# Modulation rows of a hybrid diffusion block: the four products of a weight tile in one burst

## The chip, the core and the metric

The kernel runs on one core of one Trainium2 chip. The metric is the device time of one launch, in microseconds (us). Profiles are one execution each, taken by the hardware profiler.

## What is computed

One layer of a hybrid step over 384 tokens (128 context, 256 latent) of width 2048, all in fp32. Cut to what matters here:

```python
mod_ctx = silu(c_ctx) @ ada_w + ada_b          # ada_w: 2048 x 6144
mod_lat = silu(c)     @ ada_w + ada_b
shift, scale, gate = split(mod, 3)             # 2048 columns each
h   = rmsnorm(x, norm_g) * (1 + scale) + shift
z   = h @ w_in                                 # the big projection, 2048 x 20864
...                                            # two-way scans (branch A), short convolution (branch B)
out = (sigmoid(m_a) * (y_a @ w_out_a) + sigmoid(m_b) * (y_b @ w_out_b)) @ w_o
x   = x + gate * out                           # then a last norm
```

The change touches only the first two lines, the products of the two conditioning rows with `ada_w`: the shift and scale columns in the prologue, the gate columns near the end.

## The kernel before

**Two rows against a wide matrix.** The two conditioning rows, as columns, are the stationary operand: `cw[:, k, :]` is 128 x 32, of which two columns are used. The moving operand is a loaded tile `raw` of `ada_w`, 512 rows by 512 columns (1 MiB), that is four row blocks of 128. The product of row block k goes to the PSUM rows 32*(k % 4) and up, so to one of four 32-column parts of the PE array. The four partial sums (16 row blocks, four in each part) lie under each other in one PSUM bank. One ACT copy brings them out into `m5` (L278), `ada_b` comes in as row 98 by a POOL DMA (L268), and a later small matmul with a selector adds the rows up.

**`ada_rows` (L263)** is a generator for 512 columns. It has eight steps; a step makes the products of two row blocks, and every second one takes a new tile by `get`. One fp32 product appears in the trace as two matmul records, so a step of two products is a row "x4".

**The prologue (L348)** runs nine rounds g of eight steps j. Round g computes the shift and scale of 256 channels (four tiles, 4 MiB of `ada_w`, buffers for five tiles), loads two row blocks of six column tiles of `w_in` (`early_load`, j = 5, 768 KiB) and, for the channels of the round before, forms two row blocks of h: `make_h` at j = 0 and j = 2. Six products per row block of h (`early_mm`, three fp32r matmuls each, L81 to L83) are queued to be due four steps later, and `pops(2)` takes up to two of them at the end of each step. With this, no queued product is due in step j = 3 of a round, so the products of steps j = 3 and j = 4 stand next to each other on PE: row blocks on parts 2 and 3, then on parts 0 and 1.

**The order of PE is written by hand** (`manual_schedule`): PE executes matmuls in the order of the program text. The other engines and the DMA queue of SyncE (SP) are ordered by a planner. Nearly all loads go through SP, in one queue, and an SP instruction that waits for a free buffer holds back those behind it.

**The stream.** After the prologue PE works through one long stream of matmul steps (three matmuls of a 128x128 weight tile each, `mm3`), between which the scans' steps are put. For the output projection of branch A (`add_oa`, eight pairs of column tiles, 256 steps) a side generator `gate_rows` (L991) is run, one of its steps every third step of the stream (L167). For each of four column groups of the gate it has twelve steps: eight of `ada_rows`, one empty, one that splits `m5` into two parts, and two that broadcast a gate row. Its tiles have three buffers and are asked for two ahead (`gate_load`).

Of the kernel before, what the change touches and what calls it, by code (L numbers as in the profile page):

```python
# [17 lines left out]
KC = 16  # L18
# [13 lines left out]

# columns of the constant array
C_ID, C_BO, C_MF, C_MB, C_SEG, C_SEL = 0, 128, 256, 384, 512, 896
# [22 lines left out]
def hybrid_step(ctx, tc, cst, x_prompt, x_sample, state_f, state_b, c, c_ctx, ada_w, ada_b, norm_g,  # L57
# [33 lines left out]

    # steps of the dense stream put between those of the scans
    PB0, PB1, H0, H1, CH0, CH1 = 14, 3, 2, 1, 2, 2
    PRO, WINDOW, FIRST, LAST = 32, 80, 28, 16

    def wload(view, k0, cols, nm):
        """rows (k0..k0+8)*128 of a weight, 256 columns, as two halves of hi and lo"""
        w = P * len(cols)
        raw = wp.tile([P, 8, w], F32, tag="raw", name=f"raw_{nm}", bufs=2)
        if cols[-1] == cols[0] + P:  # L100
            nc.sync.dma_start(raw[:], view[:, k0:k0 + 8, cols[0]:cols[0] + 256])
        else:
            for i, c0 in enumerate(cols):
                nc.sync.dma_start(raw[:, :, i * P:(i + 1) * P], view[:, k0:k0 + 8, c0:c0 + P])
        res = [split(raw[:, 4 * q:4 * q + 4, :], [P, 4, w], "whi", "wlo", wp, f"{nm}_{q}") for q in range(2)]
        return res


    # The products with the big weights form one stream of column pairs. Its weights are loaded and split
    # half a pair ahead; a step of it is the three matmuls of one 128x128 tile.  # L110
    class Stream:
# [21 lines left out]
        def run(self):  # L133
            p = 0
            while True:
# [13 lines left out]
                for half in range(2):  # L149
                    self.load(2 * p + half)  # L150
                    self.load(2 * p + half + 1)
                    wt = self.ready.pop(2 * p + half)
                    self.ready[2 * p + half] = None
                    for q in range(2):
                        hi, lo = wt[q]
                        for i in range(nt):
                            sl = slice(i * P, (i + 1) * P)
                            for kk in range(4):
                                k = 8 * half + 4 * q + kk
                                mm3(ps[i], hi[:, kk, sl], lo[:, kk, sl], xh[k], xl[k],  # L160
                                    k == 0, k == KC - 1)
                                if half == 1 and q == 1 and kk == 3:
                                    consume(i, ps[i])
                                    if i == nt - 1:
                                        self.done.add(tag)
                                self.cnt += 1
                                if self.side is not None and self.cnt % 3 == 0:  # L167
                                    if next(self.side, 0) == 0:
                                        self.side = None
                                yield 1  # L170
# [12 lines left out]

# [1 line left out]
    class Rows:  # L185
        """[128, 16, 384] in four tiles, each given up by itself"""
        def __init__(self, pool, tag, nm):
# [51 lines left out]

    # silu of the conditioning rows, transposed, split, and put beside each other as stationary columns  # L240
    sgr = pp.tile([32, P], F32, tag="sgr", name="sgr")
# [21 lines left out]
    def ada_rows(cw, m5, cols, ps, get):  # L263
        """both conditions times 512 columns of ada_w in four partial sums, one in each 32 columns of the array
        (rows 32j and 32j+1), and ada_b under them, in eight steps"""
        o = 0
        for c0, w in cols:
            nc.gpsimd.dma_start(m5[NSEL - 1:NSEL, o:o + w], ada_b[0:1, c0:c0 + w])  # L268
            o += w
        for j in range(8):  # L270
            if j % 2 == 0:
                raw = get(j // 2)
            for kk in range(2):
                k = 2 * j + kk
                g = 32 * (k % 4)
                TE.matmul(ps[g:g + 32, 0:512], cw[:, k, :], raw[:, k % 4, :], start=k < 4, stop=k >= KC - 4)  # L276
            if j == 7:
                S.copy(m5[0:NSEL - 1, :], ps[0:NSEL - 1, 0:512])  # L278
            yield 1
# [22 lines left out]

    # the first six column tiles take the row blocks of h as these come: the low-rank inputs (three), r, k and v
    # of block 0
    ecols = ((O_WD, 3 * P), (O_R, P), (O_K, P), (O_V, P))
# [42 lines left out]
    for g in range(9):  # L348
# [5 lines left out]
        for j in range(8):  # L354
            if g < 8:
                next(steps)
# [7 lines left out]
            if g == 0 and j == 3:  # L364
                # x rows normalised to unit mean square
                junk = pp.tile([P, 512], F32, tag="junk", name="junk")
# [16 lines left out]

# [1 line left out]
    ya_d = dp.tile([NB, P, T], F32, tag="ya_d", name="ya_d")  # L385
# [6 lines left out]

# [1 line left out]
    r_, k_, v_, ga_ = {}, {}, {}, {}  # L394
# [5 lines left out]
    def shift(dst, z, ci, mp, mn, rows=P, copy=True):  # L400
        """dst = z*(1-mu_p-mu_n) + mu_p*previous + mu_n*next, context and latent tokens apart"""
        r = slice(0, rows)
# [28 lines left out]
    def add_gv(b):  # L431
        """gate of block b, v of block b+1"""
        def consume(i, ps):
            if i == 0:
                take_gate(b, ps)
            else:
                take_shifted("v", 32, v_, b + 1, ps)
        cols = (O_GA + P * b, O_V + P * (b + 1)) if b < NB - 1 else (O_GA + P * b,)
        ds_.add(f"gv{b}", win, cols, hx, consume)
# [3 lines left out]

    # branch B: gated short convolution
    cc, uu = {}, {}
# [41 lines left out]

    # projection of branch B, gated, through the space of h
    wob = w_out_b[0].rearrange("(k p) n -> p k n", p=P)
# [40 lines left out]

# [1 line left out]
    ctx_sc = ExitStack()  # L532
    sp = ctx_sc.enter_context(tc.tile_pool(name="sp", bufs=1))
    box["sp"] = sp

    # low-rank inputs: wd forward, wd backward, ad forward, ad backward; the backward ones in reversed time
    l_hi = sp.tile([96, 4, T], F32R, tag="l_hi", name="l_hi")
# [25 lines left out]

    # states and the padded decays live in fixed places: zeros and ones in them are written once
    st = {}
# [37 lines left out]
    def prep_a(b, o):  # L603
        """decays, rates and keys of heads 2b, 2b+1"""
        bs = slice(b * P, (b + 1) * P)
# [48 lines left out]
    def prep_b(b, o):  # L654
        """the decayed operands and the masked matrices inside the chunks"""
        r, kk = r_[b], o["kk"]
# [18 lines left out]
        for d in range(2):  # L675
# [14 lines left out]
            for e in range(2):  # L690
                es = slice(32 * e, 32 * e + 32)
                nc.sync.dma_start(ui[d, e].rearrange("i s t -> s i t"),
                                  A[es, :, :, es].rearrange("s n h t -> s (n h) t"))
        # inversion of the 32x32 diagonal blocks, an instance on each partition
        U = sp.tile([48, 32, 32], F32, tag="U", name=f"U_{b}")
# [25 lines left out]
    def prep_c(b, o):  # L721
        """keys and values by token, the values' part of the removals, the bonus"""
        r, v = r_[b], v_[b]
# [18 lines left out]
        for d in range(2):  # L742
            bt = sp.tile([P, NCH, P], F32, tag=f"bt{d}", name=f"bt_{b}_{d}")
            # the last latent chunk changes no state that is read
            for n0, n1 in (((0, 3), (3, 5)), ((0, 3), (4, 6)))[d]:
# [28 lines left out]
    def scan(b, o):  # L774
        # upper right blocks of the 64x64 inverses, U11*A12*U22; the first product transposed
        for d in range(2):
# [83 lines left out]
        while live:  # L860
            k = 0
            for ch in list(live):
# [6 lines left out]
                if k == 2 or (k and ch is live[-1]):  # L869
                    yield CH0 if len(live) > 2 else CH1  # L870
                    k = 0
        # reads within the chunks, both directions summed
        py = bank(f"py2_{b}")
# [8 lines left out]
        V.tensor_tensor(ytok[:], ytok[:], py[:, 0:3, :], ALU.add)  # L882
        # final context states
        for d in range(2):
# [7 lines left out]
    def norm(b, o):  # L892
        """group norm of a block's reads"""
        ytok = o["ytok"]
# [14 lines left out]
    def finish(b, o):  # L909
        """its affine part, bonus and gate, by channel"""  # L910
        py = bank(f"py_{b}")
# [51 lines left out]

# [1 line left out]
    og = ctx.enter_context(tc.tile_pool(name="og", bufs=1))  # L965
# [25 lines left out]
    def gate_rows():  # L991
        """gate rows, broadcast over the partitions"""
        for q in range(4):
# [54 lines left out]
    def res_cols(s, j, c0, w, ps):  # L1048
        """residual of w columns: x + gate*out, its squares, its product with final_g"""
        ns = slice(c0, c0 + w)  # L1050
# [6 lines left out]
    for nq in range(3):  # L1057
# [19 lines left out]
        for s in range(3):  # L1077
            res_cols(s, nq, 512 * nq, 512, acc[s][:])
    # the last columns, token tile by token tile
    rsf = op.tile([P, 3, 3], F32, tag="rsf", name="rsf")  # L1080
# [60 lines left out]
```

## Time and profile before

| | |
|---|---|
| time, median of 3 runs | 2334.06 us (2333.88 to 2334.62) |
| span of the profiled execution | 2333.0 us |
| PE busy | 2295.7 us (98%) |
| DVE busy / ACT busy | 1568.7 us (67%) / 1120.9 us (48%) |
| HBM traffic | 336.7 MB, 144 GB/s over the span |
| PE records of the prologue's rows (L276, `pada`) | 256 |
| PE records of the gate's rows (L276, `pg`) | 128 |

The span runs from the first to the last instruction; the time lies 1.1 us above it. PE is the engine of which a whole-span share says most, but shares are means over stages: the prologue (to about 154 us), the scans with the stream (to about 1960 us), the projections (to the end) have to be read apart.

### The profile page before, as it was taken

What the parts mean: (1) busy time and instruction counts of PE and PEld (TensorE: products, weight loads), DVE (VectorE), ACT (ScalarE), POOL (GpSimd) and SP (SyncE); (2) the same over time, 40 slices, a digit from 0 to 9 for tenths busy, and PEclk for the clock granted to TensorE, in tenths of its full rate; (3) what the DMA queues carried; (4) which work ended last, traced back from release to release, by engine and by line L of the source; (5) the groups of instructions that cost most, each with busy time, mean ns of one, the idle gap of its engine ahead of it and who ended that gap; (6) DMA issues with size and microseconds to landing.
All of it is one profiled execution on the core that took longest, in us unless ns stands there. A gap on an engine that the chain in (4) does not pass through costs nothing.

```text
span 2333.0 us, 42495 instructions
## 1 busy us (share of the span) xinstructions
PE 2295.7 (98%) x16788; PEld 2043.7 (88%) x16788; DVE 1568.7 (67%) x3350; ACT 1120.9 (48%) x2342; POOL 81.6 (3%) x83
## 2 busy tenths in 40 slices
PE   5999999999999999999999999999999999999998
PEld 2579999989898989899998989898989989868988
DVE  2258777787777878787877777776868665333444
ACT  3246445454555555464645464555555543223333
POOL 2000000000000000000000000000000000000000
PEclk9999999999999999999999999999999999999999
DMA  9963433434353434343433444343444457774633
GB/s 335 344 177 106 128 103 107 134 101 126 103 138 94 124 106 127 99 121 104 130 105 107 141 116 137 109 140 100 131 118 130 144 175 243 239 257 154 226 133 119
DMA packets 431718, 340.08 MB, mean 146 GB/s; under 512 B 84816, under 2 KB 413088, under 8 KB 430624
## 3 DMA queue, kind: packets, MB, share of 16 engines
q1 hardware_dynamic: 430032, 335.62, 48.2%
q8 instruction: 132, 2.16, 0.4%
q10 hardware_dynamic: 432, 1.57, 0.2%
q14 instruction: 66, 0.54, 0.1%
q0 software_dynamic: 1056, 0.19, 0.1%
HBM read 307.37 MB, written 29.36 MB: 144 GB/s over the span
## 4 chain that ended last, share of the span: by engine, by line
PE 95%; DVE 1%; DMA 1%; SPq 1%; issue 1%; ACT 0%; POOLq 0%; POOL 0%; ACTq 0%
PE d_rk L81 4%; PE d_rk L83 4%; PE d_rk L82 4%; PE d_gv L81 3%; PE d_gv L82 3%; PE d_gv L83 3%; PE d_ma L81 3%; PE d_bc L81 3%; PE d_mb L81 2%; PE d_bg L81 2%; PE d_bx L81 2%; PE d_gb L81 2%; PE pA L684 2%; PE d_oa L81 2%; PE pada L276 2%; PE d_oa L83 2%
## 5 line engine op out<-in xcount | busy, mean ns | idle before, releaser
L701 DVE TENSOR_TENSOR ut<-U 48x30 f32<-48x30 f32 (+14 forms) x480 | 154.3, 322 | 60.6 <-DMA U<-ui 49.5
L81 PE MATMUL d_gv<-h_hi,whi_gv 128*128 128x384 f32 x496 | 165.9, 335 | 0.0
L83 PE MATMUL d_gv<-h_hi,wlo_gv 128*128 128x384 f32 x496 | 165.7, 334 | 0.0
L82 PE MATMUL d_gv<-h_lo,whi_gv 128*128 128x384 f32 x496 | 165.7, 334 | 0.0
L81 PE MATMUL d_rk<-h_hi,whi_rk 128*128 128x384 f32 x480 | 160.6, 335 | 0.6 <-ACT lst L542 0.6
L82 PE MATMUL d_rk<-h_lo,whi_rk 128*128 128x384 f32 x480 | 160.3, 334 | 0.0
L83 PE MATMUL d_rk<-h_hi,wlo_rk 128*128 128x384 f32 x480 | 160.3, 334 | 0.0
L703 DVE TENSOR_TENSOR U<-U,ut 48x30 f32<-48x30 f32 (+14 forms) x480 | 153.8, 320 | 8.9
L88 ACT CAST whi_gv<-raw_gv 128x1024 fp32r<-128x1024 f32 (+1 forms) x64 | 65.7, 1027 | 138.0 <-PE d_rk L82 96.6
L88 ACT CAST whi_rk<-raw_rk 128x1024 fp32r<-128x1024 f32 x60 | 62.9, 1050 | 112.1 <-PE d_rk L82 35.2
L838 ACT ACTIVATE ls<-st,ep 64x64 f32<-64x64 f32 x256 | 88.5, 346 | 52.3 <-DVE st L855 30.5
L89 DVE TENSOR_TENSOR wlo_rk<-raw_rk,whi_rk 128x1024 fp32r<-128x1024 f32 x60 | 73.2, 1220 | 46.3 <-ACT whi_rk L88 46.1
L89 DVE TENSOR_TENSOR wlo_oa<-raw_oa,whi_oa 128x1024 fp32r<-128x1024 f32 x32 | 39.2, 1224 | 91.0 <-ACT whi_oa L88 91.0
L81 PE MATMUL d_bc<-h_hi,whi_bc 128*128 128x384 f32 x256 | 96.9, 379 | 0.0
L81 PE MATMUL d_ma<-h_hi,whi_ma 128*128 128x384 f32 x256 | 96.8, 378 | 0.0
L81 PE MATMUL d_mb<-h_hi,whi_mb 128*128 128x384 f32 x256 | 96.6, 377 | 0.0
L81 PE MATMUL d_gb<-h_hi,whi_gb 128*128 128x384 f32 x256 | 96.1, 375 | 0.0
L81 PE MATMUL d_bx<-h_hi,whi_bx 128*128 128x384 f32 x256 | 95.2, 372 | 0.0
L844 ACT COPY sav<-pq 64x64 f32<-64x64 f32 x384 | 79.4, 207 | 32.9 <-PE pq L842 25.1
L81 PE MATMUL d_bg<-h_hi,whi_bg 128*128 128x384 f32 x256 | 95.0, 371 | 0.0
L81 PEld LDWEIGHTS d_gv<-h_hi,whi_gv 128*128 128x128 f32 x496 | 93.1, 188 | 0.2
L82 PEld LDWEIGHTS d_gv<-h_lo,whi_gv 128*128 128x128 f32 x496 | 93.1, 188 | 0.0
(317 smaller groups left out, 6726.4 us busy)
## 6 DMA issues: line engine op xcount, KB each, us to landing
raw_adah<-in_ada_w_dram SPq DMA_DIRECT2D x64, 512.0 KB, 8.0
raw_gv<-in_w_in_dram SPq DMA_DIRECT2D x62, 512.0 KB, 4.4
raw_rk<-in_w_in_dram SPq DMA_DIRECT2D x60, 512.0 KB, 5.3
raw_bc<-in_w_in_dram SPq DMA_DIRECT2D x16, 1024.0 KB, 5.4
raw_bx<-in_w_in_dram SPq DMA_DIRECT2D x16, 1024.0 KB, 5.5
raw_bg<-in_w_in_dram SPq DMA_DIRECT2D x16, 1024.0 KB, 5.5
raw_gb<-in_w_in_dram SPq DMA_DIRECT2D x16, 1024.0 KB, 5.4
raw_ma<-in_w_in_dram SPq DMA_DIRECT2D x16, 1024.0 KB, 5.4
```

Of the source, the lines that this page charges most:

```text
L81: TE.matmul(out, wh, xh, start=start, stop=False)
L82: TE.matmul(out, wh, xl, start=False, stop=False)
L83: TE.matmul(out, wl, xh, start=False, stop=stop)
L88: S.copy(hi[0:rows], src)
L89: V.tensor_tensor(lo[0:rows], src, hi[0:rows].bitcast(F32), ALU.subtract)
L276: TE.matmul(ps[g:g + 32, 0:512], cw[:, k, :], raw[:, k % 4, :], start=k < 4, stop=k >= KC - 4)
L684: TE.matmul(pas[h][:, n, :], bk[hss[h], n3 + n, :], pr[hss[h], n3 + n, :], start=True, stop=True)
L701: V.tensor_tensor(tv, U[:, 0:s, s:s + 1].broadcast_to([48, s, w]), U[:, s:s + 1, s + 1:].broadcast_to([48, s, w]), ALU.mult)
L703: V.tensor_tensor(U[:, 0:s, s + 1:], U[:, 0:s, s + 1:], tv, ALU.add)
L838: S.mul(ls[hss[h], :], s_[hss[h], hss[h]], lam[hss[h]])
L844: S.copy(sav[0:C, n, hss[h]], pq[hss[h], 0, 0:C])
```

## The change

`ada_rows` has four steps in place of eight. A step takes one tile and issues the products of its four row blocks, one on each column part, with nothing between them. In the prologue the steps are taken at j = 1, 3, 5 and 7 only. For the gate the side generator, which now has eight steps per column group, is run every fifth step of the stream in place of every third. The number of products, their operands and the loads are the same. Docstrings and comments are taken out as well.

```diff
@@ class Stream, run()
-                                if self.side is not None and self.cnt % 3 == 0:
+                                if self.side is not None and self.cnt % 5 == 0:
@@ def ada_rows(cw, m5, cols, ps, get):
         for c0, w in cols:
             nc.gpsimd.dma_start(m5[NSEL - 1:NSEL, o:o + w], ada_b[0:1, c0:c0 + w])
             o += w
-        for j in range(8):
-            if j % 2 == 0:
-                raw = get(j // 2)
-            for kk in range(2):
-                k = 2 * j + kk
-                g = 32 * (k % 4)
-                TE.matmul(ps[g:g + 32, 0:512], cw[:, k, :], raw[:, k % 4, :], start=k < 4, stop=k >= KC - 4)
-            if j == 7:
+        for j in range(4):
+            raw = get(j)
+            for kk in range(4):
+                k = 4 * j + kk
+                TE.matmul(ps[32 * kk:32 * kk + 32, 0:512], cw[:, k, :], raw[:, kk, :], start=j == 0, stop=j == 3)
+            if j == 3:
                 S.copy(m5[0:NSEL - 1, :], ps[0:NSEL - 1, 0:512])
             yield 1
@@ prologue, for j in range(8):
-            if g < 8:
+            if g < 8 and j % 2 == 1:
                 next(steps)
             if j == 0 and g == 0:
                 nc.sync.dma_start(xt[:, 0, :], x_prompt[0])
```

## Rows read from the trace of the kernel before

**Rows 1.** The page: busy time per engine, share of the span, instructions.

```profile
PE 2295.7 (98%) x16788; PEld 2043.7 (88%) x16788; DVE 1568.7 (67%) x3350; ACT 1120.9 (48%) x2342; POOL 81.6 (3%) x83
```

**Rows 2.** Busy time by stretch; after the engines: granted clock, DMA share, GB/s.

```profile
14.00:31.00 17.00, 6.24 (x27) 1.14 (x27) 5.68 (x6) 8.45 (x22) 0.89 (x1) 1.00 1.08 349
...
60.00:90.00 30.00, 30.00 (x159) 15.96 (x155) 6.91 (x18) 8.07 (x12) 1.92 (x4) 1.00 1.10 345
90.00:120.00 30.00, 30.00 (x158) 16.34 (x157) 7.98 (x17) 6.42 (x11) 1.76 (x4) 1.00 1.09 341
120.00:130.00 10.00, 10.00 (x51) 5.66 (x50) 2.87 (x5) 2.57 (x4) 0.16 (x1) 1.00 1.03 318
...
200.00:1960.00 1760.00, 1757.70 (x13900) 1619.87 (x13899) 1327.78 (x2972) 931.92 (x2060) 61.05 (x34) 1.00 0.43 122
...
2016.00:2126.00 110.00, 110.00 (x535) 74.71 (x534) 35.08 (x44) 28.51 (x38) 0.97 (x2) 1.00 0.73 243
```

**Rows 3.** Timeline of PE in the gate's stage: start, duration, instruction.

```profile
2056.93 1.05 PE L276 MATMUL pg<-raw_adag,condw_gate 128*32 128x512 f32 x4
...
2059.70 1.05 PE L276 MATMUL pg<-raw_adag,condw_gate 128*32 128x512 f32 x4
...
2067.93 0.33 PE L81 MATMUL d_oa<-yah,whi_oa 128*128 128x384 f32 x1
...
2069.49 0.33 PE L81 MATMUL d_oa<-yah,whi_oa 128*128 128x384 f32 x1
```

**Rows 4.** The gate's PSUM tile, all its matmul records.

```profile
L276 PE MATMUL pg<-raw_adag,condw_gate x128: 592/605/617, 2016.4 to 2124.5; 128*32 128x512 f32 x128
```

**Rows 5.** Timeline of PE in the prologue, rounds 2 to 4.

```profile
54.93 1.06 PE L276 MATMUL pada<-raw_adah,condw_pro 128*32 128x512 f32 x8
...
57.17 1.05 PE L276 MATMUL pada<-raw_adah,condw_pro 128*32 128x512 f32 x4
...
59.39 1.05 PE L276 MATMUL pada<-raw_adah,condw_pro 128*32 128x512 f32 x4
...
63.83 1.05 PE L276 MATMUL pada<-raw_adah,condw_pro 128*32 128x512 f32 x4
...
79.76 1.05 PE L276 MATMUL pada<-raw_adah,condw_pro 128*32 128x512 f32 x4
```

**Rows 6.** Waits of the SP queue, 20 to 125 us: total, times, longest.

```profile
SPq L259 <- PE pada L276: 20.2, 13, 3.6
```

**Rows 7.** Timeline of SP, and the landing of the last issue of that row.

```profile
122.79 0.97 SPq L259 DMA_DIRECT2D raw_adah<-in_ada_w_dram  x2
...
raw_adah<-in_ada_w_dram SPq DMA_DIRECT2D x1, 512.0 KB, 8.0
```

**Rows 8.** Timeline of PE at the end of the prologue.

```profile
141.19 1.05 PE L276 MATMUL pada<-raw_adah,condw_pro 128*32 128x512 f32 x4
...
147.98 0.44 PE L82 MATMUL pe<-h_lo,ehi 128*128 128x384 f32 x1 [0.64 <-DVE h_lo L339]
```

**Rows 9.** The copy out of the partial sums, all eight rounds.

```profile
L278 ACT COPY m<-pada x8: 585/586/587, 30.6 to 142.3; 98x512 f32<-98x512 f32 x8
```

**Rows 10.** End of the prologue: timeline of ACT, SP's issues, the second one's landing.

```profile
142.77 2.00 ACT L88 CAST whi_rk<-raw_rk 128x1024 fp32r<-128x1024 f32 x2
...
123.86 4.10 SPq L104 DMA_DIRECT2D raw_rk<-in_w_in_dram  x2
...
raw_rk<-in_w_in_dram SPq DMA_DIRECT2D x1, 512.0 KB, 8.4
```

**Rows 11.** DMA issues of the gate's stage: count, KB each, median us to landing.

```profile
raw_adag<-in_ada_w_dram SPq DMA_DIRECT2D x13, 1024.0 KB, 5.3
```

**Rows 12.** Waits of the SP queue, gate's stage: total, times, longest.

```profile
SPq L259 <- PE pg L276: 54.7, 13, 5.1
SPq L101 <- DVE wlo_oa L89: 19.6, 6, 8.6
```

**Rows 13.** Timeline of PE in round 1, just after its long waits.

```profile
31.72 1.92 PE L276 MATMUL pada<-raw_adah,condw_pro 128*32 128x512 f32 x4 [0.32 <-DMA raw_adah<-in_ada_w_dram]
```

## Prediction

> **What bounds the kernel now.** I read the page first: PE is busy for 98% of the span [rows 1], so the order of PE's work is the time, and what leaves PE comes off the end if no other engine or transfer is late in its place. Then the busy time by stretch, because the change lies in two stages only. In the long middle, 200 to 1960 us, PE is busy 1757.70 of 1760 us [rows 2]: whatever is gained ahead of it is carried through, since PE waits for nothing there. In the gate's stage PE is fully busy and the DMA share is 0.73. In the prologue from 60 to 120 us PE is full as well, but so is the DMA: share 1.09 to 1.10 at 341 to 345 GB/s [rows 2]. Two resources are full there at once, and the shorter one's saving ends at the other. That is what the reader should see before any sum is made.
>
> **The price of a burst.** The gate's stage gives it with its surroundings. Where a burst stands among nine stream matmuls, the period is 2059.70 - 2056.93 = 2.77 us; nine matmuls alone take 2069.49 - 2067.93 = 1.56 us [rows 3]. A burst of two products therefore costs 1.21 us all in: its own time, the change of array shape and the slower neighbours. What four products cost, this trace shows already: in the prologue two steps stand together once a round, on all four parts. That burst is 1.06 us long (x8), the others 1.05 us (x4), and from its start to the next burst, with six matmuls between, it is 57.17 - 54.93 = 2.24 us against 59.39 - 57.17 = 2.22 us [rows 5]. Two more products cost 0.02 us.
>
> The Trainium skill's page "TensorE: Matmul & The Clock Gate", Part 3, section "Measured speedup vs the span model", speaks against so free a lunch: four tiles packed in the rows of the array gave it 3.07 times one, not four times. By that a burst of four would take 4/3.07 = 1.3 times one product, an estimate of 0.3 us more on each 1.05 us, 5 us over the gate's 16 bursts, and the sum would come out near 2310 us. The x8 row disagrees.
>
> **The gate, term by term.** The tile pg has 128 records, four to a burst: 32 bursts [rows 4]. 16 remain. Saved: 16 x 1.21 = 19.4 us; added: 16 x 0.02 = 0.3 us. Net 19.0 us, all on PE's path. The side steps go from 48, every third stream step (144 steps), to 32, every fifth (160 steps); both fit into the 256 steps of this projection, so nothing runs over its end. The empty step, the split and the selector products stay, with more stream between split and use. Nothing is late next if the tiles are there: a tile is released by one burst in place of two, the load three tiles on is then issued, lands 5.3 us later (median) [rows 11], and is wanted three intervals on. An interval becomes five stream steps and a burst, 5 x 0.52 + 1.23 = 3.8 us (0.52 is a third of 1.56), so 11.5 us ahead, where it was 6 x 0.52 + 2 x 1.21 = 5.5 us and 16.6 us ahead. The bytes are the same in 19 us less of the 110 us stretch: 243 GB/s [rows 2] becomes 243 x 110/91 = 294 GB/s, below the 345 that the prologue draws. I cost this at nothing; without that cover see the second rival.
>
> **The prologue, PE's side.** A round takes 79.76 - 63.83 = 15.93 us [rows 5]. It has seven separate bursts (six of two, one of four) and would have four. One costs 2.22 us less six matmuls (6/9 of 1.56 = 1.04 us) = 1.18 us. PE's round falls by 3 x 1.18 = 3.5 us to 12.4 us.
>
> **The prologue, the DMA's side.** A round loads 4 MiB and 768 KiB, 4.98 MB by the code; at 345 GB/s that is 14.4 us. This is more than 12.4, so PE will now wait for tiles, some 2 us a round, and the DMA is the bound. What the prologue gains is the distance that PE had fallen behind the loads by its end. The last half tile is issued at 123.25 (the second of the x2 row) and lands 8.0 us later, at 131.2 [rows 7]; PE's last burst starts only at 141.19 [rows 8]. The queue itself was held back a little by PE: 20.2 us of waits for buffers in 13 pieces [rows 6], which show in the rate only late (341 GB/s from 90 us, 318 from 120 [rows 2]). Regained at 345: 30 x 4/345 + 10 x 27/345 = 1.1 us at most; I take 0.7. The last burst then starts at 130.5 in place of 141.19: 10.7 us. After it come the same products and two `make_h`, in the same order.
>
> **What is moved.** The copy of the partial sums had a burst and six matmuls before the products that need it, now six matmuls (1.04 us) and three transposes; it takes 0.59 us [rows 9], and remains hidden. On SP the loads of x (3 MiB, 9 us at 349 GB/s [rows 2]) pass ahead of the first tile, whose burst comes that much later; all tiles behind keep their places, so the queue's end does not move. The order of `early_load` against the third and fourth tile is unchanged. The bias DMAs on POOL are issued a step later, a round ahead of their use. One thing can be late next: on ACT the splits of the stream's first weights (2.00 us at 142.77) are put ahead of `make_h`'s work, and their data lands at 126.15 + 8.4 = 134.5 [rows 10]. The issue at 126.15 is the second of that row. With the last burst at 130.5 ACT would wait to about 133.8 and be free at 135.8, 5.3 us after the burst, where it was 144.77 - 141.19 = 3.6 us. PE already lost 0.64 us there [rows 8]. Bounds: 0.6 us gained, if the planner puts the splits behind; 1.7 us lost. I take 1.0 lost, as the order of the trace is the nearest row. The prologue gives 9.7 us.
>
> **Sum.** 2333.0 - 19.0 - 9.7 = 2304.3 us of span; the time lies 1.1 us above the span (2334.06 against 2333.0), so **2305.4 us**.
>
> **The rivals.**
> First, the tile loads of the gate come late. On SP they stand between loads of the stream's weights, which waited up to 8.6 us for a buffer [rows 12]. 8.6 + 5.3 = 13.9 us is 2.4 us more than the 11.5 us that remain. Against it: that buffer comes free by PE's own progress, which is faster too, and before the change no tile was late. For two or three such meetings 6 us: 2311 us.
> Second, slower than before: PE falls to its low clock in the prologue and stays there. At 31.72, after the stretch 14 to 31 us in which PE was busy 6.24 of 17 us [rows 2], a burst took 1.92 us [rows 13], 1.83 times the later 1.05. The granted clock of that stretch reads 1.00, which is the level of 2.4 GHz, so only the durations tell. If the new waits kept PE there, a round would take 12.4 x 1.83 = 22.7 us, 6.8 more than now; from four of the seven full rounds on the loss exceeds the gate's 19.0 us and the rest, and with all seven it is 48 - 19 = 29 us: 2363 us. Against it: PE would idle 2 of 14.4 us, not 10.8 of 17, and the rows after 31.72 returned to 1.05 us while such waits still went on.
> The Trainium skill's page "TensorE: Matmul & The Clock Gate", Part 1, states that the clock is halved while the engine has been idle and comes back with activity. The durations agree (1.92, then 1.05 us); the granted clock in the rows doesn't show it.
> Third, the change doesn't do what it says: four products cost twice two. Then only the slower neighbours are saved, 16 x (1.21 - 1.05) = 2.6 us, and nothing in the prologue: 2331.5 us. The x8 row stands against it.
> Fourth, the loads are no bound, and PE saves 7 x 3.5 = 24.8 us in the prologue: 2290 us. It needs more than the 345 GB/s at which the queue ran for 60 us.
>
> **Chances and range.** Forecast 0.81; late gate loads 0.11; low clock 0.03; four as dear as two 0.03; loads no bound 0.02. The forecast's own bounds: the gate's net 15 to 19.4, the prologue 8 to 11.4, so 2303.3 to 2311.1. The range takes these and the first rival, and some for a planner that orders ACT and DVE anew: 2301 to 2312. A measurement of this kernel can tell 0.2% (4.7 us) from no change. Faster by more: forecast, late loads and free loads with a remainder, 0.95. Within: 0.02. Slower: 0.03.
>
> **What would show it.** Right: rows of x8 with about 1.06 us in both stages, 16 of them for `pg`, and the gate's bursts with their neighbours 16 times 1.23 us; PE waiting on the tile loads up to 2 us a round, its last prologue burst at 130 to 131 us, DMA at 345 GB/s to there. Wrong: bursts near 2 us, a wait of PE for `raw_adag`, or the last burst past 133 us. The forecast fails if the loads slow down when PE reads in denser bursts, or if the tail after 130.5 stretches.

## The result, and the profile after

The kernel after takes **2308.59 us** (median of 4 runs, 2307.03 to 2310.09) against 2334.34 us of the kernel before in the same session (median of 4): a ratio of 0.9887, 95% interval 0.9873 to 0.9901. The forecast was 2305.4 us, in a range of 2301 to 2312. The time lies in the range, 3.2 us above the forecast. The profiled execution took 2310.09 us, the longest of the four, with a span of 2308.3 us, so the span moved by 24.7 us where 28.7 were forecast.

The stages show where that came from. They are cut at three instructions of PE: the first stream matmul (`d_rk`), the first matmul of the gate's projection (`d_oa`) and the first of the last projection (`acc`).

| stage of the profiled execution | before, us | after, us | difference | forecast |
|---|---|---|---|---|
| prologue, to the first `d_rk` | 154.93 | 149.83 | -5.10 | -9.7 |
| stream and scans, to the first `d_oa` | 1860.88 | 1860.53 | -0.35 | 0 |
| gate's projection, to the first `acc` | 175.89 | 156.69 | -19.20 | -19.0 |
| last projection, to the end | 141.27 | 141.27 | 0.00 | 0 |

The gate came out as worked out. The prologue gave only half. First the views that answer to those of before. The page's row of PE, and then the busy time by stretch (columns as in [rows 2]; in 2010 to 2101 us lies the gate's stage, which is shorter now):

```profile
PE 2261.6 (98%) x16788; PEld 2045.1 (89%) x16788; DVE 1568.8 (68%) x3350; ACT 1122.9 (49%) x2342; POOL 81.7 (4%) x83
```

```profile
60.00:90.00 30.00, 26.31 (x165) 17.00 (x164) 8.54 (x18) 8.43 (x12) 1.92 (x4) 0.94 1.08 340
90.00:120.00 30.00, 26.42 (x175) 17.90 (x174) 8.62 (x20) 8.43 (x12) 1.92 (x4) 1.00 1.10 345
120.00:130.00 10.00, 9.49 (x61) 6.11 (x60) 2.47 (x9) 3.62 (x5) 0.00 (x0) 1.00 1.11 338
130.00:142.00 12.00, 8.54 (x44) 6.42 (x45) 6.48 (x11) 5.46 (x8) 0.00 (x0) 0.85 0.58 154
142.00:154.00 12.00, 11.39 (x57) 11.07 (x57) 3.54 (x10) 4.27 (x11) 2.40 (x10) 0.87 0.37 101
200.00:1960.00 1760.00, 1758.01 (x13888) 1620.63 (x13889) 1328.01 (x2972) 930.46 (x2055) 61.08 (x34) 1.00 0.43 123
2010.00:2101.00 91.00, 91.00 (x536) 74.20 (x535) 35.80 (x45) 28.65 (x37) 0.97 (x2) 1.00 0.87 292
```

Before, PE and DMA were both full from 60 to 120 us [rows 2]. Now PE has slack there (26.31 and 26.42 of 30 us) and the DMA has not: 340 and 345 GB/s. The instructions of PE are as many as before (16788), but its busy time fell by 34 us: a burst of two had kept PE busy as long as one of four does. In the gate's stage PE is still full and the loads run at 292 GB/s, close to the 294 of the forecast. New is a granted clock (the column behind POOL's) below 1.00: 0.94 in the row from 60 us, 0.85 and 0.87 in the two rows from 130 us on.

Now the gate, on PE's timeline and with all its records (answers to [rows 3] and [rows 4]; L274 is the matmul that was L276):

```profile
2045.84 1.07 PE L274 MATMUL pg<-raw_adag,condw_gate 128*32 128x512 f32 x8
...
2049.67 1.06 PE L274 MATMUL pg<-raw_adag,condw_gate 128*32 128x512 f32 x8
```

```profile
L274 PE MATMUL pg<-raw_adag,condw_gate x128: 592/604/617, 2011.5 to 2103.5; 128*32 128x512 f32 x128
```

The bursts are x8 and 1.06 us long, so 16 of them hold the 128 records. From one to the next, with 15 stream matmuls between, it is 2049.67 - 2045.84 = 3.83 us; the 15 take 5 x 0.52 = 2.60, which leaves 1.23 us for a burst with its neighbours, the number forecast.

The prologue on PE's timeline (answers to [rows 5] and [rows 8]; the last column is the idle time before the instruction and who ended it):

```profile
74.00 1.94 PE L274 MATMUL pada<-raw_adah,condw_pro 128*32 128x512 f32 x8 [3.50 <-DMA raw_adah<-in_ada_w_dram]
...
88.12 1.06 PE L274 MATMUL pada<-raw_adah,condw_pro 128*32 128x512 f32 x8 [0.19 <-DMA raw_adah<-in_ada_w_dram]
...
97.35 1.06 PE L274 MATMUL pada<-raw_adah,condw_pro 128*32 128x512 f32 x8
102.61 1.06 PE L274 MATMUL pada<-raw_adah,condw_pro 128*32 128x512 f32 x8 [1.88 <-DMA raw_adah<-in_ada_w_dram]
...
111.86 1.06 PE L274 MATMUL pada<-raw_adah,condw_pro 128*32 128x512 f32 x8
116.91 1.07 PE L274 MATMUL pada<-raw_adah,condw_pro 128*32 128x512 f32 x8 [1.70 <-DMA raw_adah<-in_ada_w_dram]
...
131.48 1.90 PE L274 MATMUL pada<-raw_adah,condw_pro 128*32 128x512 f32 x8 [1.99 <-DMA raw_adah<-in_ada_w_dram]
...
141.31 0.44 PE L82 MATMUL pe<-h_lo,ehi 128*128 128x384 f32 x1 [1.98 <-DVE h_lo L337]
...
149.83 0.45 PE L81 MATMUL d_rk<-h_hi,whi_rk 128*128 128x384 f32 x1 [0.61 <-ACT lst L540]
```

A round now takes 116.91 - 102.61 = 14.3 us (it was 15.93, forecast 14.4), with one wait of 1.7 to 1.9 us on a tile, as forecast. What PE and the SP queue waited for, in total, in pieces, and the longest (SP from 20 to 125 us, as in [rows 6]):

```profile
PE pada L274 <- DMA raw_adah<-in_ada_w_dram: 25.4, 9, 10.6
...
PE pe L82 <- DVE h_lo L337: 2.0, 1, 2.0
```

```profile
SPq L259 <- PE pada L274: 3.0, 5, 1.0
```

The queue waits 3.0 us for buffers in place of 20.2 [rows 6]: PE no longer holds the loads back. But there are two surprises at the end of the prologue. The last burst takes 1.90 us, not 1.06, and PE then waits 1.98 us for `h_lo`, where it was 0.64 [rows 8]. The granted clock by stretches of 2 us tells what the first of these is (columns as in [rows 2]):

```profile
74.00:76.00 2.00, 2.00 (x9) 0.34 (x9) 0.54 (x1) 0.01 (x1) 0.00 (x0) 0.50 1.08 342
76.00:78.00 2.00, 2.00 (x12) 1.97 (x12) 0.00 (x0) 0.57 (x1) 0.00 (x0) 0.76 1.09 350
...
132.00:134.00 2.00, 2.00 (x10) 0.70 (x3) 0.00 (x0) 0.58 (x1) 0.00 (x0) 0.50 0.69 182
134.00:136.00 2.00, 2.00 (x13) 1.97 (x13) 0.00 (x0) 1.05 (x2) 0.00 (x0) 0.75 1.15 323
...
142.00:144.00 2.00, 2.00 (x8) 2.00 (x8) 0.97 (x2) 0.00 (x0) 0.00 (x0) 0.50 0.85 247
144.00:146.00 2.00, 2.00 (x10) 2.00 (x9) 0.00 (x0) 0.00 (x0) 0.00 (x0) 0.69 1.02 268
```

From 60 us on PE is granted half of its clock three times (0.50, the level of 1.2 GHz), each time just behind a wait: of 3.50 us before 74.00, of 1.99 before 131.48, of 1.98 before 141.31. The Trainium skill's page "TensorE: Matmul & The Clock Gate", Part 1, section "What's actually happening", says that half the clock is the default: a PE that has been idle runs at 1.2 GHz until it has been active for a while. These rows agree on the two levels and on the order. Not every wait is followed by it: behind the 1.88 us before 102.61 the clock stayed at 1.00.

### The profile page after: what moved, and what is told of

Same layout as the page of the kernel before. It is cut to its first block, busy times and chain, and to the rows that moved or that the text cites. A ratio compares the mean times of both kernels' runs of the same rounds, so it can differ in the third digit from the quotient of the medians.

```text
span 2308.3 us, 42501 instructions
## 1 busy us (share of the span) xinstructions
PE 2261.6 (98%) x16788; PEld 2045.1 (89%) x16788; DVE 1568.8 (68%) x3350; ACT 1122.9 (49%) x2342; POOL 81.7 (4%) x83
## 3 DMA queue, kind: packets, MB, share of 16 engines
q10 hardware_dynamic: 432, 1.57, 0.2%
## 4 chain that ended last, share of the span: by engine, by line
PE 93%; SPq 2%; DMA 2%; DVE 2%; issue 1%; ACT 0%; POOLq 0%; POOL 0%; ACTq 0%
PE d_rk L81 4%; PE d_rk L82 4%; PE d_rk L83 4%; PE d_gv L81 3%; PE d_gv L82 3%; PE d_gv L83 3%; PE d_ma L81 3%; PE d_bc L81 3%; PE d_mb L81 3%; PE d_bg L81 2%; PE d_bx L81 2%; PE d_gb L81 2%; PE pA L682 2%; PE d_oa L81 2%; PE d_bc L83 2%; PE d_ma L83 2%
```

## The experiments

Two theories stood for the 4.6 us that the prologue lacks. **A:** they are paid at the end of the prologue alone, by PE's clock behind two waits and by the longer wait for `h_lo`, which the splits of the stream's first weights delay on ACT. **B:** the two halves of the change get in each other's way, or the loads are not what sets the prologue's pace, and the gain went into something that lies in all rounds. The kernel after was not run again beside the experiments, so differences to it are taken from the ratios to the kernel before, each of which has an interval of about 3 us.

### One half of the change alone

```diff
@@ e1_prologue_only: the gate keeps its eight steps of two products and its cadence
-                                if self.side is not None and self.cnt % 5 == 0:
+                                if self.side is not None and self.cnt % 3 == 0:
-            yield from ada_rows(cw2, m5, gcols[q], pa, get)
+            yield from ada_rows8(cw2, m5, gcols[q], pa, get)   # as before the change
@@ e2_gate_only: the prologue keeps its eight steps
-            if g < 8 and j % 2 == 1:
+            if g < 8:
-            steps = ada_rows(condw, m5, ac, pa, ...)
+            steps = ada_rows8(condw, m5, ac, pa, ...)
```

> The burst of four in the prologue alone; the gate keeps eight steps, one every third stream step. Theory A (the two stages add up: the prologue gives what its end moved in the trace of after, 154.93 to 149.83 us, and nothing of it is lost later): 2334.3 - 5.1 = 2329.2 us, the stream's first matmul near 149.8 us. Rival B (the forecast's 9.7 us were gained and something in the scans took half back): the stream's first matmul is again near 149.8, but with the gate as before the time is not 5.1 us below before; or it lies at 145 us. Either shows as a total other than 2328.5 to 2330.

> The burst of four for the gate alone, one every fifth stream step; the prologue keeps its bursts of two. Theory A: the projection with the gate takes 156.7 us in place of 175.9 (16 bursts of 1.21 us fewer), 2334.3 - 19.2 = 2315.1 us, PE waits for no gate tile. Rival B (the stages interact, part of the gain at the gate comes from the shifted prologue): under 17 or over 21 us.

The prologue alone took 2328.82 us (ratio 0.9970, 0.9958 to 0.9982), that is -6.7 us; the gate alone 2316.0 us (0.9918, 0.9904 to 0.9931), -19.5 us; the kernel before stood at 2335.52. The sum, -26.2, is what both did together (2335.52 x (1 - 0.9887) = 26.4). Within these intervals the halves don't touch each other, and the gate's projection took 156.69 us in the trace of the second, to the digit as in the kernel after. In the trace of the first the stream started at 147.96 us, not near 149.8: the 5.1 us that its expectation took from the one trace of the kernel after are not fixed (the last table below).

### Does the clock cost it: matmuls that fill the two waits

```diff
+    def filler(n, w, nm):
+        f = pps.tile([P, 512], F32, tag="tr", name=nm)
+        for i in range(n):
+            TE.matmul(f[:, 0:T], w[0][:, i % 2, 0:P], h_hi[0], start=True, stop=True)
+            if g == 7 and j == 7:
+                filler(12, hlp, "fill_a")     # ahead of the last burst
+                if e[0] == 14 and e[2] == 0:
+                    filler(13, e[1], "fill_b")     # ahead of the products that wait for h_lo
```

> After, with matmuls without use put into PE's two last waits of the prologue: 12 fp32r matmuls ahead of the last burst, 13 ahead of the products of row block 14, each 0.173 us, results read by nobody. Theory A (in these waits PE falls to its low clock and pays 0.84 + 0.76 us at the last burst and 1.57 us behind the second wait): the last burst takes 1.06 us again, the matmuls behind it 0.17 us apart, and the stream starts 3.2 us earlier, near 146.6; time 2308.6 - 3.2 = 2305.4. Rival B (the records are slow there because the loads of the next weights disturb PE's reads, the clock is only reported): the burst stays at 1.9 us, no gain, or a loss of up to 1 us from the fillers.

In the prologue it went as theory A says, but the time did not: 2311.79 us (0.9897, 0.9884 to 0.9911), about 2.3 us over the kernel after where 3.2 less were expected. PE's timeline:

```profile
129.20 2.26 PE L344 MATMUL fill_a<-h_hi,ehi 128*128 128x384 f32 x12
131.40 1.06 PE L274 MATMUL pada<-raw_adah,condw_pro 128*32 128x512 f32 x8
...
146.60 0.45 PE L81 MATMUL d_rk<-h_hi,whi_rk 128*128 128x384 f32 x1 [0.61 <-ACT lst L550]
```

The last burst starts where it did (131.40) and takes 1.06 us, and the stream starts 3.23 us earlier than after (146.60 against 149.83). The granted clock is 1.00 there. One execution can't show that the fillers held it up, because it also stayed up once without them (the last table below). From there to 1858 us all of that stays. Then, while the last of the small triangular inverses runs, it is lost: this inverse ends 27.35 us behind the first `d_ob` matmul, in the kernel after 24.08. DVE's timeline in that stretch, first of the run with fillers, then of the kernel after:

```profile
1862.12 0.56 DVE L505 TENSOR_TENSOR ybl<-yst_b,ybh 128x384 fp32r<-128x384 f32 x1 [1.24 <-ACT ybh L504]
...
1866.28 0.56 DVE L505 TENSOR_TENSOR ybl<-yst_b,ybh 128x384 fp32r<-128x384 f32 x1 [0.27 <-ACT ybh L504]
...
1881.27 1.23 DVE L89 TENSOR_TENSOR wlo_ob<-raw_ob,whi_ob 128x1024 fp32r<-128x1024 f32 x1 [2.20 <-ACT whi_ob L88]
```

```profile
1881.28 1.22 DVE L89 TENSOR_TENSOR wlo_ob<-raw_ob,whi_ob 128x1024 fp32r<-128x1024 f32 x1 [0.37 <-ACT whi_ob L88]
```

The steps of the inverse share DVE with splits, in an order that the planner makes. With the fillers it made another one, and DVE stood 1.24 + 0.27 + 2.20 = 3.71 us in place of 0.37 behind splits whose operands had not come. On PE the loss shows in two places, first of the run with fillers, then of the kernel after:

```profile
1872.89 0.44 PE L83 MATMUL d_ob<-ybh,wlo_ob 128*128 128x384 f32 x1 [1.41 <-DVE wlo_ob L89]
...
1895.23 0.39 PE L790 MATMUL pH<-x,A 32*32 32x32 f32 x24 [1.61 <-DMA x<-uo]
```

```profile
1874.73 0.44 PE L83 MATMUL d_ob<-ybh,wlo_ob 128*128 128x384 f32 x1 [1.00 <-DVE wlo_ob L89]
```

At this `d_ob` product 1874.73 - 1872.89 = 1.84 us of the gain are left, and the wait of `pH` (the products that use the inverse), 1.61 us, takes most of the rest. So a gain of 3.2 us ahead of the long middle was given back 1700 us later, and the time alone would have spoken against theory A. Why the planner's order changes so far from the place of the edit was not tried.

### Does the wait for `h_lo` cost it: the splits held back

```diff
-    def split(src, shape, th, tl, pool, nm, rows=P):
+    def split(src, shape, th, tl, pool, nm, rows=P, after=None):
+        if after is not None:
+            G.tensor_copy(hi[0:1, 0, 0:1], after)
-    ds_.load(0)
+    ds_.load(0, h_lo[15][0:1, 0:1])
```

One element of each of the first weights' high parts is first written from the last `h_lo`, so that ACT's split can't go ahead of it.

> After, with the splits of the stream's first weights held back until the last row block of h is done (a one-element POOL copy from it into the tiles that the splits write), so that ACT and DVE do the last two blocks of h first. Theory A (the second wait of 1.98 us and the low clock behind it come from these splits standing ahead): no wait of PE for h_lo, stream starts 1.98 + 1.57 = 3.5 us earlier, near 146.3; time 2305.1. The last burst stays at 1.9 us. Rival B (the splits then are late for the stream): PE waits for whi_rk or wlo_rk at the stream's start, and the gain is under 1 us.

2305.22 us (0.9871, 0.9858 to 0.9885), -3.7 us against the kernel after by the two ratios; the intervals still touch. PE's and ACT's timelines:

```profile
131.51 1.07 PE L276 MATMUL pada<-raw_adah,condw_pro 128*32 128x512 f32 x8 [0.38 <-DMA raw_adah<-in_ada_w_dram]
...
144.61 0.41 PE L81 MATMUL d_rk<-h_hi,whi_rk 128*128 128x384 f32 x1 [0.66 <-ACT lst L542]
```

```profile
137.78 0.52 ACT L338 CAST h_hi<-hf 128x384 fp32r<-128x384 f32 x1
138.20 2.96 ACT L90 CAST whi_rk<-raw_rk 128x1024 fp32r<-128x1024 f32 x3
```

The splits stand behind the last `h_hi`, the wait for `h_lo` is gone, and with it the fall of the clock behind it. The stream starts at 144.61. From the last burst to there it is 13.10 us, less even than before (154.93 - 141.19 = 13.74 us [rows 8]). In this execution the clock had fallen a round earlier (0.92 from 120 to 130 us), so that PE reached the last burst late, waited only 0.38 us and had its full clock: 1.6 of the 5.2 us are that chance, not the edit. Against an execution with the full clock at both waits (146.21 - 130.99 = 15.22 us, the last table below) the held splits save 2.1 us; what more they save is a fall of the clock that comes in some executions only.

### Held splits and a filler together

The edit of the run before, and the first group of fillers, ahead of the last burst.

> The kernel after with the splits of the stream's first weights held behind the last h_lo (as in the run that held them) and, besides, 12 full-array matmuls into an unused bank just ahead of the last prologue burst, which waits for its tile about 2 us. The run with the splits held alone happened to reach that burst only 0.4 us early and at the high clock, so its gain of 5.2 us in the stream's start held 1.6 us of luck. Theory (the low clock after a wait and the wait for h_lo are the two halves of what the prologue lacks): last burst 1.06 us long, no wait for h_lo, stream start at 144.5 +- 0.5 us, time 2303 to 2306 if the scans run as in the kernel after; the kernel with the splits held alone is not beaten by more than 1.6 us. Rival (the fillers delay the last burst themselves, or the DVE order behind them changes a later stage, as in the run with two groups of fillers, which lost 3.2 us between 1860 and 1897 us): 2306 to 2309.

The stream's start came out as expected, 144.34 us, 13.1 us behind the last burst as in the run before, and the time as the rival had it: 2307.58 us (0.9883, 0.9866 to 0.9899). Again the last inverse lost what was won (it ended 26.56 us behind the first `d_ob`; DVE stood 2.06 + 0.23 + 0.62 us behind splits there). By the medians the held splits alone stay the fastest version that computes the whole of it.

### Are the loads the bound of the prologue

```diff
+            kept = {}
+            def get(i, g=g, ac=ac, kept=kept):
+                if i % 2 == 0:
+                    kept[0] = ada_load(pp, f"h{g}", ac, i, 5)
+                return kept[0]
-            steps = ada_rows(condw, m5, ac, pa, lambda i: ada_load(pp, f"h{g}", ac, i, 5))
+            steps = ada_rows(condw, m5, ac, pa, get)
```

> The kernel after, with only the first and third tile of each prologue round loaded; the second and fourth product bursts reuse the tile before them. So half of the rows of ada_w for the shift and scale columns are left out and the output is another one; all products, splits and transposes stay. It takes 2 MiB of 4.98 MB out of each of the eight rounds. Theory (the loads set the prologue's pace after the change): PE goes at its own pace of about 12.4 us a round, the waits for these tiles (25.4 us in 9 pieces in the kernel after) all but vanish, the last burst starts near 115 us in place of 131.48, and the time falls by 15 to 20 us to 2289 to 2294. Rival (PE still sets the pace, or the freed buffers do, and the loads are hidden): last burst at 130 to 132, time 2307 to 2310.

2287.77 us (0.9795, 0.978 to 0.981), some 21 us below the kernel after. The windows (60 to 90 us) and PE's timeline:

```profile
60.00:90.00 30.00, 30.00 (x198) 19.89 (x190) 10.77 (x21) 9.82 (x15) 2.89 (x6) 1.00 0.72 226
```

```profile
97.16 1.06 PE L274 MATMUL pada<-raw_adah,condw_pro 128*32 128x512 f32 x8
...
109.65 1.06 PE L274 MATMUL pada<-raw_adah,condw_pro 128*32 128x512 f32 x8
111.90 1.06 PE L274 MATMUL pada<-raw_adah,condw_pro 128*32 128x512 f32 x8
115.20 1.07 PE L274 MATMUL pada<-raw_adah,condw_pro 128*32 128x512 f32 x8
```

PE is full again, the DMA is not (226 GB/s), a round takes 109.65 - 97.16 = 12.5 us, and the last burst starts at 115.20. The loads were the bound of the prologue after the change, and theory B falls. The fourth rival, that the loads are no bound, falls too; its 2290 us are what the kernel comes near to (2288) once half of these loads are gone.

### Why four products cost as much as two

```diff
-                TE.matmul(ps[32 * kk:32 * kk + 32, 0:512], cw[:, k, :], raw[:, kk, :], start=j == 0, stop=j == 3)
+                g, first, last = (j, kk == 0, kk == 3) if one else (kk, j == 0, j == 3)
+                TE.matmul(ps[32 * g:32 * g + 32, 0:512], cw[:, k, :], raw[:, kk, :], start=first, stop=last)
```

`one` is set for the gate alone.

> The kernel after, with the gate's bursts put on one column part each: the four products of a loaded tile add up in the same 32 columns of the array (the tile's number picks which), in place of one product in each of the four parts. Work, loads and order are the same. Theory (four products cost as much as two only because the parts run at the same time): a burst of four grows from 1.06 us to about 4 x 0.9 to 4 x 1.0 us, +2.5 to +3.0 us for each of 16 bursts, +40 to +48 us: 2349 to 2357. Rival (what a burst costs is the entry into and the exit from the narrow shape, the products inside go at a rate that does not ask for separate parts): bursts under 1.5 us, time within 7 us of 2308.6.

2348.88 us (1.0056, 1.0041 to 1.0071): slower than before the change. PE's timeline:

```profile
2046.91 3.62 PE L275 MATMUL pg<-raw_adag,condw_gate 128*32 128x512 f32 x8
...
2053.28 3.62 PE L275 MATMUL pg<-raw_adag,condw_gate 128*32 128x512 f32 x8
```

The same eight records take 3.62 us on one column part, 1.06 us on four. The gate's projection grew from 156.69 to 197.31 us, 40.6 us for 16 bursts, 2.54 us each. So the four parts work side by side, and it is this that the change uses; before it, half of them stood idle in most bursts. The Trainium skill's page "TensorE: Matmul & The Clock Gate", Part 3, section "Measured speedup vs the span model", gives 3.07 times for four tiles packed in the rows of the array. That is another packing, which no run here has; the four column parts give 3.62/1.06 = 3.4 times.

### Does the gate need the slower cadence

```diff
-                                if self.side is not None and self.cnt % 5 == 0:
+                                if self.side is not None and self.cnt % 3 == 0:
```

> The kernel after, with the gate's side step at every third stream step again, as before the change. A tile is then wanted every 3 x 0.52 + 1.23 = 2.8 us in place of 3.8 us; 1 MiB in 2.8 us is 375 GB/s, and the stream's own weights come on top. Theory (the fifth step is needed because the loads would be late at the third): PE waits for raw_adag 1 to 3 us at each group of four tiles, +2 to +8 us: 2310.6 to 2316.6. Rival (three buffers and the steps without a burst carry it): no wait for raw_adag, the gate's projection takes 156.7 us as after, time within 1 us of 2308.6.

2307.14 us (0.988, 0.9865 to 0.9895), no different from the kernel after. The rival holds: PE waits for no tile and the projection takes 156.69 us again. On PE's timeline the tiles are now wanted every 2.8 us:

```profile
2043.99 1.07 PE L274 MATMUL pg<-raw_adag,condw_gate 128*32 128x512 f32 x8
2046.78 1.06 PE L274 MATMUL pg<-raw_adag,condw_gate 128*32 128x512 f32 x8
2049.56 1.06 PE L274 MATMUL pg<-raw_adag,condw_gate 128*32 128x512 f32 x8
```

The price that I set on late tiles was wrong; that the four steps without a burst in each column group let the loads catch up is likely, and was not tried by itself. The cadence of the change gains nothing and costs nothing; the 19.2 us are the bursts' alone.

### The end of the prologue in four executions

The prologue's code of four of these kernels is the same (after, the prologue alone, the two gate experiments), so their traces are four executions of it:

| profiled execution | last burst starts | end of the wait for `h_lo` | stream starts | first stretch | second stretch |
|---|---|---|---|---|---|
| after | 131.48 | 141.31 | 149.83 | 9.83 | 8.52 |
| prologue alone | 131.18 | 141.01 | 147.96 | 9.83 | 6.95 |
| gate on one part | 131.84 | 141.67 | 148.64 | 9.83 | 6.97 |
| gate every third | 130.99 | 139.25 | 146.21 | 8.26 | 6.96 |
| before | 141.19 | 147.98 | 154.93 | 6.79 | 6.95 |
| gate alone (prologue as before) | 141.22 | 148.00 | 154.96 | 6.78 | 6.96 |

The first stretch runs from the last burst to the end of the wait, the second from there to the stream. PE's timeline of the last of the four, where the clock stayed up behind both waits:

```profile
130.99 1.06 PE L274 MATMUL pada<-raw_adah,condw_pro 128*32 128x512 f32 x8 [1.69 <-DMA raw_adah<-in_ada_w_dram]
...
139.25 0.45 PE L82 MATMUL pe<-h_lo,ehi 128*128 128x384 f32 x1 [1.68 <-DVE h_lo L337]
...
146.21 0.45 PE L81 MATMUL d_rk<-h_hi,whi_rk 128*128 128x384 f32 x1 [0.61 <-ACT lst L540]
```

The same loads run beside this burst and it takes 1.06 us, so loads that disturb PE's reads (rival B of the fillers) are not what made it 1.90 us.

Each stretch has two lengths, 1.57 us apart: 8.26 or 9.83, and 6.95 or 8.52. That is the price of one fall of the clock. In the kernel after's profiled execution it fell behind both waits, in two of the others behind the first alone, in the last behind none. The second wait was even longer where no fall came behind it, as with the prologue alone (2.10 us, and products of 0.34 us behind it):

```profile
141.01 0.44 PE L82 MATMUL pe<-h_lo,ehi 128*128 128x384 f32 x1 [2.10 <-DVE h_lo L353]
...
142.16 0.34 PE L82 MATMUL pe<-h_lo,ehi 128*128 128x384 f32 x1
```

So the change's gain in the prologue is 5.1 to 8.7 us from execution to execution of the same code: up to 3.1 us of that spread is the clock, the rest the landing of the last tile.

## Why the prediction was right, and where it was not

**The gate: right by its steps.** 16 bursts of 1.21 us less, 0.02 us more on the others: forecast 19.0, measured 19.2 us, with the 1.23 us of a burst and its neighbours found again. The run with one column part bears the step that four cost what two do.

**The late tiles of the gate (first rival): did not happen.** Even a tile every 2.8 us was in time.

**The prologue's bound: right.** The loads end the rounds (14.3 us, forecast 14.4), PE waits for one tile a round, and taking half of the loads away moved the last burst to 115 us, at 12.5 us a round where 12.4 were forecast for PE alone.

**The prologue's gain: half of what was forecast in the profiled execution,** 5.10 in place of 9.7 us. The 4.6 us are three terms. The last burst started at 131.48, not 130.5 (0.98 us): its tile lands at 130.85 to 131.70 in the seven traces with this prologue, at 131.2 before [rows 7], so the 0.7 us that I took for the queue's waits in [rows 6] never came. The queue's waits fell from 20.2 to 3.0 us and the landing did not move beyond its spread; before, the engines had been kept at a share of 1.09 to 1.10 from 60 to 120 us beside these waits [rows 2]. The tail was taken as 1.0 us longer, by the place of ACT's splits; it was 8.26 - 6.79 = 1.47 us in the execution with the full clock (0.47 us). The mechanism is the one named: held back, the splits cost nothing, and the tail came out 0.6 us shorter than before, the lower bound that stood in the text. The rest, 2 x 1.57 = 3.1 us, is the clock. One more term lies outside the stages: the sum put the time 1.1 us above the span, a median of three runs against the span of one execution; where one execution has both, it is 2310.09 - 2308.3 = 1.8 us. That the time lies in the range all the same is in part luck: 5.10 us is outside the prologue's own bounds of 8 to 11.4, and the gate, near the top of its 15 to 19.4, made room for it.

**The clock (second rival): the step that failed.** I asked whether PE would fall to the low level and stay there, found that one row of slow bursts [rows 13] was followed by fast ones, gave it 3%, and set nothing for a fall that passes. But one fall costs 1.57 us, and the profiled execution paid for two. In the rounds it is free: the slow stretch behind 74.00 us ate the next round's wait on the loads (0.19 us before 88.12 in place of 1.7 to 1.9). Behind the last load nothing is left to eat, and a fall there goes to the end. Two waits of 2 us lie there, both of which the change made or lengthened. The larger part of the price was to be had from [rows 13]: 1.92 - 1.05 = 0.87 us for the burst. In the kernel after it was 1.90 - 1.06 = 0.84 us for the last burst, and the rest of the 1.57 us for the matmuls behind it. That the first wait would come, some 2 us for the last tile, stood in the prediction; that there is a price behind it did not.

**What is gained ahead is carried through: right for this change, not in general.** From the first `d_rk` to the first `d_oa` the kernel after lost nothing (-0.35 us). In both runs with fillers some 3 us were lost there, although in the prediction a PE that waits for nothing was to carry every gain through: another order on DVE made it wait anew.

**The third rival** (four cost twice two) did not happen: four cost 1.06 us. On one column part they cost more than three times that, and the time was 2349 us.

## What to carry to other kernels

When an edit turns a full PE into one that waits for loads, look at the last wait: in the rounds a slow restart is hidden by the next wait, behind the last load each one that comes costs about 1.6 us here, and each wait that the edit moves there is itself paid in full. A product that uses 32 of the array's columns should go out four at a time, one on each column part: four cost 1.06 us, two cost 1.05. Read a gain by stages, not by the time: three microseconds won in the prologue were lost to a planner's order 1700 us later, and only the stages showed both.

## What was not expected of the hardware

- Of waits of 1.7 to 2.1 us in the same code some were followed by a fall of the clock that cost 1.57 us and some were not: behind the wait for `h_lo` one of 1.98 us was (kernel after), one of 2.10 us was not (prologue alone). So the length of the wait alone does not decide it; what does is left open.
- The granted clock of the profile shows these falls, in stretches of 2 us: 0.50. In a stretch of 30 us around one it reads 0.94. It does not show the slow bursts at the start: in the kernel before it reads 1.00 in the 2 us that hold most of the burst at 31.72 [rows 13], which took 1.92 us. There the durations alone tell, as the prediction said.

```profile
32.00:34.00 2.00, 2.00 (x9) 0.43 (x5) 0.51 (x4) 0.00 (x0) 0.00 (x0) 1.00 1.09 348
```

- Loads of 1 MiB every 2.8 us for four tiles in a row beside the stream's own weights (307 GB/s over the gate's 73 us) made no tile late.
